# Attention of a four-layer hybrid model: GpSimd takes the low parts of half of each weight chunk and the zero blocks

## The chip, the cores and the metric

The kernel runs on one core of a Trainium2 chip. The metric is the device time of one execution in microseconds (us), as the median of several runs; lower is better.

The names used below: TensorE (PE in the profile) multiplies matrices, VectorE (DVE) and ScalarE (ACT) work element by element, GpSimd (POOL) can do so too, and SyncE (SP) issues the transfers from HBM. Each engine takes its instructions strictly in the order of its own queue, and waits at an instruction until the semaphores that it names have been reached.

## The reference

A model of four layers over 256 rows of 1024 columns: mixers of three kinds (retention, a gated linear recurrence, latent attention, retention again), each followed by a layer norm, and an MLP with squared ReLU, also followed by a layer norm. The change touches the third mixer alone, the latent attention:

```python
def mla_mixer(x, positions, w_in, q_norm_g, kv_norm_g, w_uq, w_ukv, w_o):
    c_q, c_kv, k_pe = jnp.split(x @ w_in, [384, 640], axis=-1)
    q = (rms_norm(c_q, q_norm_g) @ w_uq).reshape(B, S, 8, 192)
    q = jnp.concatenate([q[..., :128], rope(q[..., 128:], positions)], -1) * (192 ** -0.5)
    kv = (rms_norm(c_kv, kv_norm_g) @ w_ukv).reshape(B, S, 8, 256)
    k_nope, v = kv[..., :128], kv[..., 128:]
    k = jnp.concatenate([k_nope, broadcast(rope(k_pe, positions))], -1)
    ...                      # causal softmax(q k^T) v for each of 8 heads
    return o @ w_o
```

## The kernel before

**Numbers in two parts.** All arrays are 32-bit floats. For TensorE each operand x is split into a high part (a cast to the engine's own 32-bit format, `fp32r`) and a low part, x minus the high part. A product is then three products, added up in PSUM: high x high, high x low, low x high (`mm3`, L148 to L150). So each weight that comes from HBM costs a cast and a subtraction before it can be used. `split` (L141) does both: ScalarE casts (L142), VectorE subtracts (L143).

**Weight chunks.** `chunk` (L122) loads a piece of a weight array into one of three `raw` tiles (128 partitions x up to 2048 columns) by one transfer from SyncE's queue, and splits it into one of five `hl` tiles in two halves, first the first half of the columns, then the second. A `raw` tile can be loaded again only when both subtractions of the chunk that it held are done. In the attention a key/value chunk (`mla_ukv`, two of them) and an output chunk (`mla_o`, four) have 2048 columns, so halves of 1024; the chunk for the rotary part of the queries (`mla_uqr`, `wqr` in the code) and the two for the rest of the queries (`mla_uqn`, called uqn0 and uqn1 here) have 1536, so halves of 768. The chunks of the projection (`mla_in`, four) have 1408, halves of 704. `self.hold` orders a weight subtraction on VectorE behind an operation of the layer norm.

**The attention, `mla` (L686).** Rows come in two tiles t of 128. `down(t, i)` projects (tiles `low`) and normalises: ScalarE squares and sums (L719), VectorE scales the sum (`ve`, L165), GpSimd raises it to the power -1/2 (`rs`, L166, `rstd`), VectorE multiplies (`cn`, L721) and, for i = 0, adds the rotary terms of the keys (L726 to L730). `turn(t, i)` transposes `cn` on TensorE and splits it into `cT` (L744, L745). `values`, `keys` and `queries` make `vv`, `kn` and `qn` from `cT` and the chunks; `rope(t, w)` makes the rotary part of the queries (`qy`, then split as `qr`), and `turn_q` transposes it into `qpe`. `scores(h)` makes a head's scores `s` (L824) and its softmax (L826 to L830), `turn_p` transposes them into the tile `PT`, `attend` multiplies by the values (`oT`), and `out` multiplies by the output chunks into the accumulators `acc`. `PT` holds a block of zeros in each of its four parts (L704) for the half of the scores that the causal mask removes, and `kpe` two smaller ones (L706).

**What lies around it.** The end of the MLP before it (`close`) normalises both row tiles: the power for a row tile stands on GpSimd between the two steps L292 and L293 on VectorE. The transposes of row tile 1 (`flush`, L266) come between the projections of tile 0 and tile 1. GpSimd's only work in the whole kernel is the power of `rstd`, 36 times. The order on each engine is set by a scheduler that works on the code as it is written, so instructions of neighbouring steps are interleaved.

## Time and profile before

| | |
|---|---|
| median of 3 runs | 1321.05 us (1320.05 to 1322.92) |
| the profiled execution | 1322.59 us |
| its span, first to last instruction | 1320.8 us |
| mean granted TensorE clock | 0.997 of full speed |
| busy: TensorE, VectorE, ScalarE, GpSimd | 1303.6, 956.6, 658.9, 26.0 us |
| attention, about | 667 to 747 us of the span |

The profile shows one execution. Times inside it count from the span's start. A busy TensorE is not one at its peak, as products overlap and their ends are modelled; idle time in front of a product, with what released it, is what tells of lost time. In a row of the timeline, start and duration come first, in brackets behind it the idle time of the engine just before and what ended it; rows of the same kind are merged (x2, x3), with the time from the first start to the last end and the shape of the first of them.

### The profile page before, as it was taken

How to read it: one execution, taken by the hardware profiler on the slowest of the kernel's cores; microseconds unless marked ns; L12 is line 12 of the kernel's file. 1: busy time of each engine (PE TensorE's matmuls, PEld its weight loads, DVE VectorE, ACT ScalarE, POOL GpSimd, SP SyncE). 2: the span in 40 equal slices, each digit the busy share in tenths (PEclk: the TensorE clock that was granted, in tenths of full speed). 3: DMA queues.
4: the chain of work that ended last, by engine and by line, in shares of the span. 5: the costliest groups of instructions: out<-in, count | busy, mean ns of one | idle time of the engine just before them, and what ended most of it. 6: DMA issues, size and time to landing. Idle time of an engine off the chain costs nothing.

```text
span 1320.8 us, 17993 instructions
## 1 busy us (share of the span) xinstructions
PE 1303.6 (99%) x7130; PEld 1130.1 (86%) x7130; DVE 956.6 (72%) x1490; ACT 658.9 (50%) x1026; POOL 26.0 (2%) x40
## 2 busy tenths in 40 slices
PE   9999999999999999999999999999999999999997
PEld 6888888888889978888888888888898888888886
DVE  6976678766678988666589886666786657876664
ACT  5654445444438945444357554444444445454440
POOL 0000000000000000000010000000000000000000
PEclk9999999999999999999999999999999999999999
DMA  7745544655544366555435365555554544465540
GB/s 286 285 163 191 187 164 160 225 193 190 193 159 166 128 238 240 191 192 191 151 114 203 130 237 192 191 191 192 186 206 174 188 156 177 154 236 189 194 143 32
DMA packets 37281, 243.59 MB, mean 184 GB/s; under 512 B 4311, under 2 KB 4812, under 8 KB 10188
## 3 DMA queue, kind: packets, MB, share of 16 engines
q1 hardware_dynamic: 37196, 242.43, 51.8%
q8 instruction: 56, 0.92, 0.3%
q14 instruction: 29, 0.24, 0.1%
HBM read 241.36 MB, written 1.05 MB: 184 GB/s over the span
## 4 chain that ended last, share of the span: by engine, by line
PE 90%; DVE 5%; ACT 3%; issue 1%; DMA 0%; SPq 0%; POOL 0%; DVEq 0%; POOLq 0%; ACTq 0%
PE wk L960 14%; PE acc L148 12%; PE acc L150 12%; PE acc L149 12%; PE wk L148 10%; PE wk L150 10%; PE wk L149 10%; PE wk L962 8%; DVE hl L143 2%; PE wk L266 1%; ACT hl L142 1%; PE wk L428 1%; DMA raw<-ret_vg 0%; PE wk L984 0%; DVE Q L615 0%
## 5 line engine op out<-in xcount | busy, mean ns | idle before, releaser
L143 DVE TENSOR_TENSOR hl<-raw,hl 128x1024 fp32r<-128x1024 f32 (+3 forms) x448 | 526.3, 1196 | 176.8 <-ACT hl L142 173.8
L142 ACT CAST hl<-raw 128x1024 fp32r<-128x1024 f32 (+3 forms) x448 | 447.0, 1033 | 307.7 <-PE acc L150 174.1
L148 PE MATMUL acc<-hl,hT 128*128 128x512 f32 x512 | 200.5, 392 | 0.0
L149 PE MATMUL acc<-hl,hT 128*128 128x512 f32 x512 | 200.1, 391 | 0.0
L150 PE MATMUL acc<-hl,hT 128*128 128x512 f32 x512 | 199.2, 389 | 0.0
L960 PE MATMUL wk<-xT,hl 128*128 128x512 f32 x832 | 197.6, 390 | 0.0
L960 PEld LDWEIGHTS wk<-xT,hl 128*128 128x128 f32 x832 | 155.9, 188 | 32.3
L148 PE MATMUL wk<-hl,xT 128*128 128x512 f32 (+1 forms) x432 | 159.0, 368 | 0.3 <-ACT xT L142 0.3
L149 PE MATMUL wk<-hl,xT 128*128 128x512 f32 (+1 forms) x432 | 157.0, 364 | 0.2 <-DVE hl L143 0.2
L150 PE MATMUL wk<-hl,xT 128*128 128x512 f32 (+1 forms) x432 | 157.0, 364 | 0.0
L948 ACT COPY tb<-wk 128x256 f32<-128x256 f32 x104 | 38.8, 373 | 156.3 <-PE wk L962 156.3
L150 PEld LDWEIGHTS acc<-hl,hT 128*128 128x128 f32 x512 | 96.1, 188 | 20.3
L148 PEld LDWEIGHTS acc<-hl,hT 128*128 128x128 f32 x512 | 96.3, 188 | 18.5
L149 PEld LDWEIGHTS acc<-hl,hT 128*128 128x128 f32 x512 | 96.3, 188 | 17.9
L962 PEld LDWEIGHTS wk<-xT,hl 128*128 128x128 f32 x832 | 106.7, 191 | 4.1
L962 PE MATMUL wk<-xT,hl 128*128 128x256 f32 x832 | 107.9, 283 | 0.0
L949 DVE TENSOR_TENSOR s<-wk,tb 128x256 f32<-128x256 f32 x104 | 44.1, 424 | 80.5 <-ACT tb L948 76.8
L148 PEld LDWEIGHTS wk<-hl,xT 128*128 128x128 f32 x432 | 81.7, 189 | 14.8 <-ACT xT L142 2.6
L150 PEld LDWEIGHTS wk<-hl,xT 128*128 128x128 f32 x432 | 81.6, 189 | 14.0 <-DVE xT L143 1.6
L149 PEld LDWEIGHTS wk<-hl,xT 128*128 128x128 f32 x432 | 81.9, 190 | 12.8 <-DVE hl L143 1.1
L150 PE MATMUL wk<-xT,hl 128*128 128x256 f32 x288 | 81.6, 284 | 0.1
L148 PE MATMUL wk<-xT,hl 128*128 128x256 f32 x288 | 81.5, 283 | 0.0
(231 smaller groups left out, 1786.0 us busy)
## 6 DMA issues: line engine op xcount, KB each, us to landing
raw<-mlp SPq DMA_DIRECT2D x64, 1024.0 KB, 4.8
raw<-mlp_1b SPq DMA_DIRECT2D x56, 1024.0 KB, 4.8
raw<-ret_vg SPq DMA_DIRECT2D x30, 1024.0 KB, 4.8
raw<-ret_qk SPq DMA_DIRECT2D x16, 1024.0 KB
raw<-ret_o SPq DMA_DIRECT2D x16, 1024.0 KB, 5.0
raw<-lru_in SPq DMA_DIRECT2D x10, 1024.0 KB, 4.8
raw<-mlp_1a SPq DMA_DIRECT2D x8, 1024.0 KB
raw<-lru_o SPq DMA_DIRECT2D x5, 1024.0 KB, 4.7
```

The costliest lines, as they stand in the source:

```text
L142: self.nc.scalar.copy(out=hi, in_=x)
L143: return self.nc.vector.tensor_sub(out=lo, in0=x, in1=hi.bitcast(F32))
L148: mm(out, lhsT=st[0], rhs=mv[0], start=start, stop=False)
L149: mm(out, lhsT=st[0], rhs=mv[1], start=False, stop=False)
L150: mm(out, lhsT=st[1], rhs=mv[0], start=False, stop=stop)
L266: nc.tensor.transpose(ps[:, k * 128:k * 128 + 128], self.h[t][:, (j * 4 + k) * 128:(j * 4 + k + 1) * 128], self.idn)
L428: nc.tensor.transpose(tp[:, b * 128:b * 128 + 128], Y[h, t][:, b * 128:b * 128 + 128], self.idn)
L948: nc.scalar.copy(out=tb, in_=ps_lo)
L949: nc.vector.tensor_add(out=s, in0=ps_hi, in1=tb)
L960: mm(ps[b], lhsT=w[:, 0, k, f], rhs=xT[:, k], start=k == 0, stop=False)
L962: mm(ps[b][:, 256:], lhsT=w[:, 1, k, f], rhs=xT[:, k, 0], start=False, stop=k == 7)
```

## The change

`chunk` and `split` get an argument that puts the subtraction of a chunk's last half on GpSimd; the cast stays on ScalarE and the first half on VectorE. All nine chunks of the attention behind the projection use it: two key/value, three query and four output chunks. A subtraction on GpSimd isn't ordered behind the layer norm (`hold`). The six zero blocks are written by GpSimd too.

```diff
--- before.py
+++ after.py
@@ -119,7 +119,9 @@
         return [[self.acc.tile([128, 512], F32, name=f"acc{t}{n}", tag=f"acc{t}{n}") for n in range(2)]
                 for t in range(2)]
 
-    def chunk(self, src, k, n, pieces=2, loads=1, hold=True, mid=None):
+    def chunk(self, src, k, n, pieces=2, loads=1, hold=True, mid=None, pool=False):
+
+
 
         nc = self.nc
         raw = self.raw.tile([128, 2048], F32, name="raw", tag="raw")
@@ -133,14 +135,15 @@
                 mid()
         step = w // pieces
         for a in range(0, w, step):
-            lo = self.split(hl[:, 0, a:a + step], hl[:, 1, a:a + step], raw[:, a:a + step])
-            if hold and self.hold:
+            by = nc.gpsimd if pool and a + step == w else None
+            lo = self.split(hl[:, 0, a:a + step], hl[:, 1, a:a + step], raw[:, a:a + step], by)
+            if hold and self.hold and not by:
                 self.after(lo, self.hold)
         return hl[:, :, :w].rearrange("p s (k n) -> p s k n", n=n)
 
-    def split(self, hi, lo, x):
+    def split(self, hi, lo, x, by=None):
         self.nc.scalar.copy(out=hi, in_=x)
-        return self.nc.vector.tensor_sub(out=lo, in0=x, in1=hi.bitcast(F32))
+        return (by or self.nc.vector).tensor_sub(out=lo, in0=x, in1=hi.bitcast(F32))
 
     def mm3(self, out, st, mv, start, stop):
 
@@ -701,9 +704,9 @@
             vv = [p.tile([128, 2, MH * MV], F32R, name=f"vv{t}") for t in range(2)]
             for n in range(2):
                 for s in range(2):
-                    nc.vector.tensor_scalar_mul(out=PT[n][:, s, :128], in0=self.idn, scalar1=0.0)
+                    nc.gpsimd.tensor_scalar_mul(out=PT[n][:, s, :128], in0=self.idn, scalar1=0.0)
             for t in range(2):
-                nc.vector.tensor_scalar_mul(out=kpe[64:, 1, t * 128:t * 128 + 128], in0=self.idn[64:], scalar1=0.0)
+                nc.gpsimd.tensor_scalar_mul(out=kpe[64:, 1, t * 128:t * 128 + 128], in0=self.idn[64:], scalar1=0.0)
             CN, QN, R, P, OT = {}, {}, {}, {}, {}
 
             def down(t, i):
@@ -778,7 +781,7 @@
                 nc.scalar.copy(out=qpe[u][:, :, t * 128:t * 128 + 128], in_=ps.rearrange("p (h i) -> p h i", h=4))
 
             def kv_load(u):
-                return self.chunk(wkv[u], 2, 1024)
+                return self.chunk(wkv[u], 2, 1024, pool=True)
 
             def values(u, w, t):
                 c = slice(t * 128, t * 128 + 128)
@@ -852,7 +855,7 @@
                 self.proj(acc, t, terms, n == 0, n == MH // 2 - 1, ns)
 
             def out_load(n):
-                return self.chunk(wo[n], 2, 1024)
+                return self.chunk(wo[n], 2, 1024, pool=True)
 
             wi = [self.chunk(win[u], 2, 704, hold=False) for u in range(4)]
             tables()
@@ -867,14 +870,14 @@
             kn = self.xp.tile([128, 2, MH, 256], F32R, name="kn", tag="xT")
             turn(1, 0)
             values(0, w[0], 0)
-            wr = self.chunk(wqr, 3, 512)
+            wr = self.chunk(wqr, 3, 512, pool=True)
             rope(0, wr)
             w.append(kv_load(1))
             values(1, w[1], 0)
             turn(1, 1)
             acc = self.accs()
             rope(1, wr)
-            wq = [self.chunk(wqn[0], 3, 512)]
+            wq = [self.chunk(wqn[0], 3, 512, pool=True)]
             keys(0, w[0], 0)
             turn_q(0, 0)
             turn_q(0, 1)
@@ -889,7 +892,7 @@
             scores(1)
             queries(1, wq[0])
             keys(1, w[1], 0)
-            wq.append(self.chunk(wqn[1], 3, 512))
+            wq.append(self.chunk(wqn[1], 3, 512, pool=True))
             scores(2)
             turn_p(0)
             scores(3)
```

The order of the instructions on the engines follows. On GpSimd, at the place in the program where the attention begins and after it (`rs` are the powers, `PT` and `kpe` the zero blocks, `hl` the weight halves), before:

```order
L1049 MEMSET const-uint8-127 128x1
L1053 UNCONDITIONAL_BRANCH
L166 ISA
L166 TENSOR_TENSOR rs<-ve,mhalf 128x1 x36
L1053 UNCONDITIONAL_BRANCH
```

and now (the first 15 powers end with that of row tile 0 in the layer norm before the attention):

```order
L169 TENSOR_TENSOR rs<-ve,mhalf 128x1 x15
L707 TENSOR_SCALAR PT_5979<-idn 128x128 x2
L707 TENSOR_SCALAR PT_5980<-idn 128x128 x2
L709 TENSOR_SCALAR kpe<-idn 64x128 x2
L146 TENSOR_TENSOR hl<-raw,hl 128x1024
L169 TENSOR_TENSOR rs<-ve,mhalf 128x1 x4
L146 TENSOR_TENSOR hl<-raw,hl 128x768
L146 TENSOR_TENSOR hl<-raw,hl 128x1024
L169 TENSOR_TENSOR rs<-ve,mhalf 128x1
L146 TENSOR_TENSOR hl<-raw,hl 128x768 x2
L146 TENSOR_TENSOR hl<-raw,hl 128x1024 x4
L169 TENSOR_TENSOR rs<-ve,mhalf 128x1 x16
```

The zero blocks and the half of the first key/value chunk stand ahead of the power of row tile 1 in that layer norm and of three powers of the projections; the halves of `wqr` and of the second key/value chunk stand ahead of the last power of the projections, `down(1, 1)`.

On VectorE, from the `ve` of `down(1, 1)` to the split of the first rotary queries (`cn<-low_6180` is the normalised product of `down(1, 1)`, `vv` the values, `qy` and `qr` the rotary queries), before:

```order
L165 TENSOR_SCALAR ve<-ss 128x1
L745 SCALAR_TENSOR_TENSOR cT<-wk,cols,cT 128x128
L721 TENSOR_SCALAR cn<-low_6180,rs 128x384
L143 TENSOR_TENSOR vv_5986<-wk,vv_5986 128x512
L745 SCALAR_TENSOR_TENSOR cT<-wk,cols,cT 128x128
L143 TENSOR_TENSOR hl<-raw,hl 128x1024
L741 TENSOR_TENSOR kpe<-wk,kpe 64x128
L764 TENSOR_TENSOR qy<-wk,tab 128x512
L767 TENSOR_TENSOR qy<-wk,tab 128x8x32 x2
L143 TENSOR_TENSOR vv_5986<-wk,vv_5986 128x512
L768 TENSOR_TENSOR qy<-qy 128x512
L745 SCALAR_TENSOR_TENSOR cT<-wk,cols,cT 128x128
```

and now:

```order
L168 TENSOR_SCALAR ve<-ss 128x1
L748 SCALAR_TENSOR_TENSOR cT<-wk,cols,cT 128x128
L724 TENSOR_SCALAR cn<-low_6180,rs 128x384
L146 TENSOR_TENSOR hl<-raw,hl 128x768
L748 SCALAR_TENSOR_TENSOR cT<-wk,cols,cT 128x128
L146 TENSOR_TENSOR vv_5986<-wk,vv_5986 128x512
L744 TENSOR_TENSOR kpe<-wk,kpe 64x128
L767 TENSOR_TENSOR qy<-wk,tab 128x512
L770 TENSOR_TENSOR qy<-wk,tab 128x8x32 x2
L146 TENSOR_TENSOR hl<-raw,hl 128x768
L771 TENSOR_TENSOR qy<-qy 128x512
L146 TENSOR_TENSOR vv_5986<-wk,vv_5986 128x512
```

The key/value half is gone from between, the first halves of uqn0 and uqn1 stand ahead of `qy` and of its last step, and one `cT` has moved behind `qr`, which before was followed by it and a half.

On ScalarE, behind the squares of `down(1, 1)`, before:

```order
L142 CAST hl<-raw 128x768
L740 CAST kpe<-wk 128x128
L142 CAST hl<-raw 128x768
L142 CAST vv_5986<-wk 128x512
L744 ACTIVATE cT<-wk,cols 128x128
L142 CAST hl<-raw 128x768
L142 CAST qr<-qy 128x4x64 x2
```

and now:

```order
L145 CAST hl<-raw 128x768
L743 CAST kpe<-wk 128x128
L145 CAST hl<-raw 128x768 x2
L145 CAST vv_5986<-wk 128x512
L747 ACTIVATE cT<-wk,cols 128x128
L145 CAST qr<-qy 128x4x64 x2
```

Both casts of uqn1 (the `hl` behind `kpe`) now stand ahead of `vv` and of the first `cT` of `turn(1, 1)`; before, one stood behind them.

## Rows read from the trace of the kernel before

**Rows 1.** The page's first part: busy us (share of the span), instructions.

```profile
PE 1303.6 (99%) x7130; PEld 1130.1 (86%) x7130; DVE 956.6 (72%) x1490; ACT 658.9 (50%) x1026; POOL 26.0 (2%) x40
```

**Rows 2.** Windows: stretch, length, each engine's busy us (instructions), clock, DMA.

```profile
664.00:745.00 81.00, 77.23 (x508) 70.47 (x507) 72.83 (x162) 52.95 (x115) 3.12 (x5) 1.00 0.50 172
```

**Rows 3.** TensorE's waits, 640 to 780: us, times, longest.

```profile
PE wk L148 <- ACT cT L744: 0.9, 1, 0.9
PE wk L150 <- DVE qn L143: 0.8, 1, 0.8
PE wk L835 <- DVE s L830: 0.7, 1, 0.7
PE wk L736 <- DVE cn L721: 0.5, 1, 0.5
```

**Rows 4.** VectorE's groups by shape, 640 to 780: busy us, mean ns.

```profile
L143 DVE TENSOR_TENSOR hl<-raw,hl 128x1024 fp32r<-128x1024 f32 x28 | 33.5, 1216 | 2.8 <-ACT hl L142 2.8
...
L143 DVE TENSOR_TENSOR hl<-raw,hl 128x768 fp32r<-128x768 f32 x6 | 5.6, 948 | 0.0
...
L704 DVE TENSOR_SCALAR PT<-idn 128x128 fp32r<-128x128 f32 x4 | 0.8, 207 | 0.0
...
L706 DVE TENSOR_SCALAR kpe<-idn 64x128 fp32r<-64x128 f32 x2 | 0.4, 222 | 0.0
```

**Rows 5.** Timeline of GpSimd, 668 to 690: start, us.

```profile
669.67 0.92 POOL L166 TENSOR_TENSOR rs<-ve,mhalf 128x1 f32<-128x1 f32 x1 [8.44 <-DVE ve L165]
675.07 0.55 POOL L166 TENSOR_TENSOR rs<-ve,mhalf 128x1 f32<-128x1 f32 x1 [4.48 <-DVE ve L165]
...
688.25 0.55 POOL L166 TENSOR_TENSOR rs<-ve,mhalf 128x1 f32<-128x1 f32 x1 [4.45 <-DVE ve L165]
```

**Rows 6.** Timeline of VectorE, 666 to 690.

```profile
669.44 1.41 DVE L292 SCALAR_TENSOR_TENSOR h<-h,mv,lng 128x512 f32<-128x512 f32 x2
670.76 1.41 DVE L293 SCALAR_TENSOR_TENSOR h<-h,rs,lnb 128x512 f32<-128x512 f32 x2
...
684.82 0.35 DVE L730 TENSOR_TENSOR cn<-ky 128x64 f32<-128x64 f32 x2
...
687.96 0.14 DVE L165 TENSOR_SCALAR ve<-ss 128x1 f32<-128x1 f32 x1
...
688.83 0.62 DVE L721 TENSOR_SCALAR cn<-low,rs 128x384 f32<-128x384 f32 x1 [0.47 <-POOL rs L166]
```

**Rows 7.** GpSimd's groups in the whole span: busy us, mean ns, idle before.

```profile
L166 POOL TENSOR_TENSOR rs<-ve,mhalf 128x1 f32<-128x1 f32 x36 | 25.8, 716 | 1290.0 <-DVE ve L165 1290.0
```

**Rows 8.** Timeline of TensorE, 675 to 698.

```profile
675.80 1.03 PE L266 MATMUL wk<-idn,h 128*128 128x128 f32 x8
...
693.17 0.50 PE L148 MATMUL wk<-hl,cT 128*128 128x512 f32 x1 [0.95 <-ACT cT L744]
...
695.87 0.60 PE L777 MATMUL wk<-idn,qr 128*128 128x128 f32 x4
```

**Rows 9.** Timeline of ScalarE, 682 to 692.

```profile
683.15 3.47 ACT L142 CAST hl<-raw 128x768 fp32r<-128x768 f32 x4 [0.24 <-PE low L150]
...
691.15 0.83 ACT L142 CAST hl<-raw 128x768 fp32r<-128x768 f32 x1 [0.54 <-DMA raw<-mla_uqn]
```

**Rows 10.** Timeline of VectorE, 689 to 696.

```profile
689.37 0.68 DVE L143 TENSOR_TENSOR vv<-wk,vv 128x512 fp32r<-128x512 f32 x1
...
690.22 1.22 DVE L143 TENSOR_TENSOR hl<-raw,hl 128x1024 fp32r<-128x1024 f32 x1
...
695.21 0.75 DVE L143 TENSOR_TENSOR qr<-qy,qr 128x256 fp32r<-128x256 f32 x2
```

**Rows 11.** Timeline of SyncE's queue, 680 to 698: issues of transfers.

```profile
682.82 4.44 SPq L131 DMA_DIRECT2D raw<-mla_uqn  x2
```

**Rows 12.** Timeline of VectorE, 709 to 714.

```profile
709.67 2.35 DVE L143 TENSOR_TENSOR hl<-raw,hl 128x1024 fp32r<-128x1024 f32 x2
...
713.25 0.69 DVE L143 TENSOR_TENSOR qn<-wk,qn 128x512 fp32r<-128x512 f32 x1
```

## The prediction

> **What bounds the kernel now.** The page comes first: TensorE is busy 99% of the span [rows 1]. So time can only come out of the places where TensorE waits, and the change can only reach those of the attention. In the window that holds it, 664 to 745 us, TensorE is busy 77.23 of 81 us, VectorE 72.83 and GpSimd 3.12, at a granted clock of 1.00 throughout [rows 2]: TensorE idles 3.8 us there, and that is the most the change can win (0.29% of the span). The view of who waited for whom names four waits of half a microsecond or more: 0.9 us for ScalarE's cT, and 0.8, 0.7 and 0.5 us for VectorE's qn, s and cn [rows 3]. VectorE releases these last three, 2.0 us, so it is the engine to relieve; but each of them is a place in an order, not a share of its load.
>
> **What leaves VectorE.** Nine second halves: six of 1024 columns at 1.216 us and three of 768 at 0.948, 10.1 us; and six zero blocks, 4 x 0.207 + 2 x 0.222 = 1.3 us [rows 4]. Together 11.4 us of its 72.8.
>
> **What GpSimd gets.** The trace holds no wide operation of GpSimd. Its only one, the power of one column in rstd, takes 0.55 us while VectorE stands idle for it [rows 5], where VectorE's one-column ve takes 0.14 [rows 6]. Bounds for a 1024-column half: no faster than VectorE's own 1.21 us, and no worse than that times 0.55/0.14, about 4.7 us. I take 2.3 us, near their geometric middle, and by the same factor 1.8 us for 768 columns (bounds 0.95 and 3.7): 19 us of work for an engine that idles 78. A zero block lies between VectorE's 0.2 us and the power's 0.55; I take 0.3. The Trainium skill (GPSIMD Engine Reference, Performance versus the Vector engine) calls GpSimd the wrong engine for elementwise work and gives 4.497 us for a two-input add of 2048 columns against VectorE's 2.293; scaled to 1024 columns that is an estimate of 2.25 us, and by it the sum below stays as it is. No row here shows it.
>
> **Do the two engines block each other?** GpSimd's 36 powers [rows 7] fall in two kinds: 16 take 0.92 us, all in layer norm while VectorE runs L292 on two SBUF inputs (h and the gain), and 20 take 0.55, while VectorE waits for their result [rows 5]. The one at 669.67 began 0.23 us after a pair of L292 did, each of which takes 0.7 us, and ended at 670.59, half a microsecond after the first of the pair [rows 6]. That is what a held port looks like. A half on GpSimd reads two SBUF tiles, as do the first halves left on VectorE, the second step of qy, the splits of qr and the sums into cn; operations on PSUM operands would not clash. I take sharing as the likelier case. The Trainium skill (SBUF — State Buffer, Who interferes with whom) says that a VectorE instruction with two SBUF inputs and a GpSimd one that reads SBUF exclude each other for the whole instruction. By that rule the time is the +1.7 us below, without it rival A's -1.8; the 0.92 against 0.55 agrees with it, but shows only GpSimd as the one that waits.
>
> **Place one, the start (667 to 679).** GpSimd's queue now holds the zero blocks and the half of the first key/value chunk ahead of the power for row tile 1 of the layer norm, which began at 669.67 [rows 5]. From about 667.5, when the MLP's last product ends: six zeros 1.8, half 2.3, power 0.9, so it ends near 672.5 instead of 670.59, and the two L293 behind it near 674.0 instead of 672.17 [rows 6]. Next late would be the power of the first projection at 675.07 [rows 5] and TensorE's transposes of that tile at 675.80 [rows 8]: the cover left is 0.8 us, and a half of over 3.1 us uses it up. On the other side, the last projection half no longer stands behind the layer norm on VectorE, and cn can come up to 0.5 us sooner [rows 3]. I take 0, with -0.7 and +1.0 as ends.
>
> **Place two, the queries (684 to 700).** ScalarE's four casts begin at 683.15 [rows 9]; the second of wqr ends near 684.8, the second of the other key/value chunk at 686.6. GpSimd makes these two halves before the power that began at 688.25 [rows 5]. With nothing shared: 684.8 + 1.8 + 2.3 + 0.55 = 689.45 for its end, 0.65 late. With sharing, VectorE's first halves and sums into cn, 0.95 + 1.21 + 0.35 [rows 4, 6], lie end to end with GpSimd's 4.1: 684.8 + 6.6 + 0.55, about 692.0, and cn behind it is done at 692.6 instead of 689.45 [rows 6]. VectorE stands still for it in either case, and all that leads to the turned qr is queued behind it. Before, that took 6.6 us, from vv at 689.37 to the end of qr at 695.96 [rows 10]; less the key/value half (1.22) and plus the first half of uqn1 that now stands there (0.95), it is 6.3 us. Nothing shared: 690.1 + 6.3 = 696.4, 0.4 late. Shared: 692.6 + 6.3 = 698.9, plus between 0 and 3.0 us (VectorE's two-input part of it) for GpSimd's two uqn halves; I take 0.3, near the low end since VectorE's PSUM operations fit beside GpSimd's halves, and get 699.2: **+3.2**, for TensorE, which turned qr at 695.87 [rows 8], waits there. TensorE's wait for cT moves too, inside these 3.2: the transfer of uqn1 needs wqr's raw buffer, which GpSimd frees near 686.6 to 687.6 (it was issued at 682.82 + 4.44 - 0.33 = 686.93 [rows 11], and ScalarE waited for it until 691.15 [rows 9]), and both uqn1 casts now stand ahead of vv and cT on ScalarE, so TensorE goes on at 693.4 to 694.4 instead of 693.17 [rows 8]. SP's later transfers and ScalarE's casts that wait for GpSimd to give up a buffer are those of the output chunks; the scores cover them.
>
> **Place three, the scores (711 to 714).** VectorE ran two weight halves of an output chunk at 709.67, and qn came only at 713.25 [rows 12]; TensorE stood 0.7 and 0.8 us for s and qn [rows 3]. One of the two halves goes, like all second halves before it, and TensorE itself comes 3.2 us later. Both waits go: **-1.5**. What is late next is TensorE, since none of the four waits lies behind this place.
>
> **Sum:** 0 + 3.2 - 1.5 = +1.7 us. The profiled run took 1322.59 us for a span of 1320.8; the median of the three is 1321.05, 1.54 less. I put the difference on the median: **1322.7 us**.
>
> **Rivals.** *A, nothing is shared.* Place one gives -0.7, place two +0.4, place three -1.5: -1.8, 1319.25 us. For it: the trace shows only GpSimd waiting, and half of VectorE's operations there read PSUM. Against: the 0.92 us. At the ceiling of 3.8 us it would be 1317.25. *B, GpSimd's queue becomes the bound.* If a 1024 half takes 4.7 and a 768 half 3.7 us and a zero 0.55, the first power ends near 676.4 and the chain of rstd and cn moves by 3 us; at place two 684.8 + 3 + 3.7 + 4.7 + 0.55 = 696.75, cn 697.4, qr 703.7, so +7.7 - 1.5 = +6.2, 1327.25 us. It decides from about 3.1 us for a 1024 half, where the cover of place one ends. For it: 0.55 us for one column; against: much of that must be fixed cost. *C, it does nothing.* The halves all come in time, but TensorE's next limit at each place is ScalarE's cT or a transfer, so that what is won at one is stood out at the next: 1321.05 us.
>
> **How the numbers follow.** About 0.2% (2.6 us) is what a measurement of this kernel can tell from no change. Forecast (shared, +1.7): 0.48, of which 0.35 within that bound, 0.12 slower and 0.01 faster. A: 0.32, of which 0.17 faster and 0.15 within, since its centre is close to the bound and its ceiling beyond it. B: 0.15, of which 0.14 slower. C: 0.05, within. Sums: faster 0.18, same 0.56, slower 0.26. The range, 1318.0 to 1325.6, goes from 1.2 us under A's centre to the forecast with all 3.0 us of sharing at place two, and leaves out most of B and the best end of A.
>
> **What would show it.** In the changed profile: GpSimd's 1024 halves near 2.3 us (over 3.1: B); VectorE's two-input operations stretched, or never beside a half of GpSimd (neither: A); the last power of the attention beginning near 691.5 (689: A); TensorE waiting over a microsecond before the first turn of qr; and no wait for s and qn around 711 to 717. The forecast is wrong if VectorE does not stretch, if qr comes in time, or if place three keeps its waits.

## The result, and the profile after

| | before | after |
|---|---|---|
| median | 1321.30 us (5 runs, 1320.05 to 1322.92) | 1327.97 us (5 runs, 1327.44 to 1329.58) |
| ratio | | 1.0052, interval 1.0040 to 1.0063 |
| profiled execution, its span | 1322.59, 1320.8 us | 1327.52, 1325.7 us |

The change makes the kernel 6.7 us slower. The forecast was 1322.7 us with a range of 1318.0 to 1325.6 and chances of 0.18 for faster, 0.56 for the same and 0.26 for slower: the time lies outside the range, on the side that had 0.26.

In the two profiled executions all of the difference lies in the attention. A good ruler there is GpSimd's own work: from the start of the power of row tile 0 in the layer norm ahead of it to the start of the first power behind it. In this document that is called the stretch. It leaves out what runs before and behind. GpSimd's timeline (start, us, engine, line, operation; idle time before it in brackets), before:

```profile
660.30 0.92 POOL L166 TENSOR_TENSOR rs<-ve,mhalf 128x1 f32<-128x1 f32 x1 [168.38 <-DVE ve L165]
...
750.98 0.92 POOL L166 TENSOR_TENSOR rs<-ve,mhalf 128x1 f32<-128x1 f32 x1 [62.19 <-DVE ve L165]
```

and after, which answers to [rows 5]:

```profile
659.79 0.92 POOL L169 TENSOR_TENSOR rs<-ve,mhalf 128x1 f32<-128x1 f32 x1 [168.37 <-DVE ve L168]
666.99 2.54 POOL L707 TENSOR_SCALAR PT<-idn 128x128 fp32r<-128x128 f32 x4 [6.27 <-PE acc L153]
...
671.00 2.47 POOL L146 TENSOR_TENSOR hl<-raw,hl 128x1024 fp32r<-128x1024 f32 x1
673.44 0.57 POOL L169 TENSOR_TENSOR rs<-ve,mhalf 128x1 f32<-128x1 f32 x1
...
685.27 4.62 POOL L146 TENSOR_TENSOR hl<-raw,hl 128x768 fp32r<-128x768 f32 x2 [1.07 <-ACT hl L145]
691.32 0.55 POOL L169 TENSOR_TENSOR rs<-ve,mhalf 128x1 f32<-128x1 f32 x1 [1.42 <-DVE ve L168]
...
705.25 2.69 POOL L146 TENSOR_TENSOR hl<-raw,hl 128x1024 fp32r<-128x1024 f32 x1 [6.39 <-ACT hl L145]
708.68 2.39 POOL L146 TENSOR_TENSOR hl<-raw,hl 128x1024 fp32r<-128x1024 f32 x1 [0.75 <-ACT hl L145]
...
755.84 0.99 POOL L169 TENSOR_TENSOR rs<-ve,mhalf 128x1 f32<-128x1 f32 x1 [25.82 <-DVE ve L168]
```

The stretch was 750.98 - 660.30 = 90.68 us and is 755.84 - 659.79 = 96.05: 5.4 us longer (everything before it runs 0.5 us earlier in this execution, so the spans differ by 4.9). TensorE is busy 86.91 us of it before and 87.36 after, so what grew is its idle time, from 3.8 to 8.7 us. Line numbers after are three higher than before.

What TensorE stood for, 640 to 780 us, in the view of who waited for whom (us, times, longest), answers to [rows 3]:

```profile
PE wk L739 <- DVE cn L733: 3.1, 1, 3.1
PE wk L153 <- DVE qn L146: 1.7, 1, 1.7
PE wk L780 <- DVE qr L146: 1.5, 2, 0.8
PE wk L739 <- DVE cn L724: 1.4, 2, 0.9
PE wk L151 <- ACT cT L747: 0.7, 1, 0.7
...
```

With a wait of 0.2 us for qpe that is 8.6 us, where it was 3.7. The longest wait is new: for L733, the sums of the rotary terms into `cn`, which before lasted 0.35 us [rows 6] and held up nobody. The wait for qn is the old one at place three, twice as long; the one for s is gone.

VectorE lost 11.4 us of work, yet its busy time in the attention hardly fell: 72.41 us in a window of 88 us, where it was 72.83 in one of 81 [rows 2], and over the whole stretch 79.77 us, where it was 80.62. In the windows view (stretch, length, each engine's busy us and instructions, clock, DMA):

```profile
664.00:752.00 88.00, 79.31 (x516) 71.42 (x514) 72.41 (x148) 54.20 (x117) 28.76 (x20) 1.00 0.47 161
```

The timeline of VectorE says where the relief went. Five of its rows, all of operations on two SBUF inputs:

```profile
674.04 1.41 DVE L296 SCALAR_TENSOR_TENSOR h<-h,rs,lnb 128x512 f32<-128x512 f32 x2 [2.81 <-POOL rs L169]
...
685.83 4.15 DVE L733 TENSOR_TENSOR cn<-ky 128x64 f32<-128x64 f32 x2
...
697.69 1.79 DVE L146 TENSOR_TENSOR qr<-qy,qr 128x256 fp32r<-128x256 f32 x2
...
706.44 2.11 DVE L146 TENSOR_TENSOR qr<-qy,qr 128x256 fp32r<-128x256 f32 x2
...
709.08 3.08 DVE L146 TENSOR_TENSOR hl<-raw,hl 128x1024 fp32r<-128x1024 f32 x1
```

The first waits for GpSimd's queue: its own length is that of before, but VectorE stood 2.81 us for the power that the zero blocks and a half put off to 673.44. The other four are stretched: the sums from 0.35 to 4.15 us, qr from 0.75 [rows 10] to 1.79 and 2.11, a weight half from 1.21 to 3.08. Each lies beside a half of GpSimd. What TensorE then stands for, in its own timeline, is the end of the stretched ones (of the last of them by way of the qn that is queued behind it):

```profile
690.03 0.33 PE L739 MATMUL wk<-idn,cn 128*128 128x128 f32 x1 [3.10 <-DVE cn L733]
...
699.20 0.66 PE L780 MATMUL wk<-idn,qr 128*128 128x128 f32 x4 [0.83 <-DVE qr L146]
...
708.27 1.09 PE L780 MATMUL wk<-idn,qr 128*128 128x128 f32 x8 [0.65 <-DVE qr L146]
712.81 0.39 PE L153 MATMUL wk<-kn,qn 128*128 128x256 f32 x1 [1.71 <-DVE qn L146]
```

### The profile page after: what moved, and what is told of

It is laid out like the page before. It is cut to its first block, busy times and chain, and to the rows that moved or that the text cites. A ratio compares the mean times of both kernels' runs of the same rounds, so it can differ in the third digit from the quotient of the medians.

```text
span 1325.7 us, 18007 instructions
## 1 busy us (share of the span) xinstructions
PE 1303.9 (98%) x7130; PEld 1129.8 (85%) x7130; DVE 956.1 (72%) x1475; ACT 659.9 (50%) x1026; POOL 51.8 (4%) x55
## 4 chain that ended last, share of the span: by engine, by line
PE 91%; DVE 4%; ACT 3%; issue 1%; POOL 1%; DMA 0%; SPq 0%; DVEq 0%; POOLq 0%; ACTq 0%
PE wk L963 14%; PE acc L151 12%; PE acc L153 12%; PE acc L152 12%; PE wk L151 10%; PE wk L153 10%; PE wk L152 10%; PE wk L965 8%; DVE hl L146 1%; PE wk L269 1%; ACT hl L145 1%; PE wk L431 1%; DMA raw<-ret_vg 0%; PE wk L987 0%; DVE Q L618 0%
## 5 line engine op out<-in xcount | busy, mean ns | idle before, releaser
L146 DVE TENSOR_TENSOR hl<-raw,hl 128x1024 fp32r<-128x1024 f32 (+3 forms) x439 | 518.4, 1202 | 177.0 <-ACT hl L145 173.8
```

The lines of the kernel that those rows point to most:

```text
L146: return (by or self.nc.vector).tensor_sub(out=lo, in0=x, in1=hi.bitcast(F32))
```

## The experiments

Two theories. **S**, sharing: a GpSimd half and a VectorE operation on two SBUF inputs exclude each other, so VectorE stands while GpSimd works. **Q**, the queue: nothing is shared, but GpSimd's long operations stand ahead of its powers, for which VectorE waits.

**The operations by themselves.** The stages of this kernel are fenced off from each other; in each, GpSimd and VectorE run a row of operations on tiles in SBUF (or one in PSUM) that don't depend on each other.

```diff
+ psub(3); psub(2, 768); psub(2, 256)       # GpSimd subtracts, alone
+ vsub(3); vps(3); vsc(3); vrd(3)           # VectorE alone: two SBUF inputs, PSUM + SBUF, one input, reduce
...
+ psub(4); vsub(8)                          # side by side
+ psub(4); vps(16)
+ psub(4); vsc(24)
+ psub(4); vrd(16)
+ [memset x 8 on GpSimd]; vsub(8)
+ [product with a constant x 4 on GpSimd]; vsub(8)
```

> The whole model is left out: the kernel loads x, times operations on it in stages that are fenced off from each other, and writes x out. Theory S (a GpSimd half and a VectorE operation on two SBUF inputs exclude each other): a GpSimd subtraction of 1024 columns alone takes 2.0 to 2.6 us, of 768 columns 1.5 to 1.9; a VectorE one 1.2 us alone. Side by side, four GpSimd subtractions (9 us) and eight of VectorE (9.6 us) take together 18 to 20 us, the sum of both, while beside VectorE operations that read PSUM neither side is stretched by more than 10%. Theory Q (nothing is shared, only GpSimd's queue is long): every pair of stages takes as long as its longer side, about 10 us, and each operation lasts what it lasts alone. Zero blocks by a product on GpSimd: 0.6 us for 128 columns by both; a memset is the open point: S would leave VectorE's two-input subtractions unstretched beside it if reading is what clashes.

In the one run of it, GpSimd alone took, by shape, 2338 ns for a subtraction of 1024 columns, 1799 for 768, 951 for a memset of 1024, 530 for a zero block of 128 columns and 2767 for the same product of 1024. VectorE's 8 subtractions would take 9.3 us alone, the spacing being 1.16. Side by side, GpSimd's timeline:

```profile
34.92 13.22 POOL L101 TENSOR_TENSOR g<-h,h 128x1024 fp32r<-128x1024 f32 x4 [0.19 <-SPq L113]
52.80 9.27 POOL L101 TENSOR_TENSOR g<-h,h 128x1024 fp32r<-128x1024 f32 x4 [4.66 <-SPq L115]
62.58 10.02 POOL L101 TENSOR_TENSOR g<-h,h 128x1024 fp32r<-128x1024 f32 x4 [0.52 <-SPq L117]
...
88.99 7.20 POOL L122 MEMSET m<- 128x1024 f32 x8 [0.30 <-SPq L121]
98.25 12.10 POOL L124 TENSOR_SCALAR g<-h 128x1024 fp32r<-128x1024 f32 x4 [2.06 <-SPq L123]
```

and VectorE's of the same stages:

```profile
34.88 17.75 DVE L102 TENSOR_TENSOR o<-h,h 128x1024 fp32r<-128x1024 f32 x8 [9.45 <-SPq L113]
52.76 9.66 DVE L103 TENSOR_TENSOR o<-q,h 128x512 fp32r<-128x512 f32 x16
62.54 16.72 DVE L104 TENSOR_SCALAR o<-h 128x512 fp32r<-128x512 f32 x24
...
88.96 9.17 DVE L102 TENSOR_TENSOR o<-h,h 128x1024 fp32r<-128x1024 f32 x8
```

The first pair takes 17.8 us where the two rows alone take 9.3 + 9.3: S, if a little under its 18 to 20. While GpSimd worked, VectorE finished four of its subtractions, at a mean of 3357 ns, which is about one of each in turn: each waits for nearly the whole of the other's instruction. Beside operations that read PSUM (the second stage) nothing is stretched, nor in the fourth, not among the rows, beside VectorE's reductions (680 ns each, 674 alone). The third stage was a surprise: a product with a constant, one SBUF input, went from 416 to 771 ns at the mean, 16.7 us for 24. And in the fifth GpSimd's writes, 7.20 us of them, cost VectorE's subtractions nothing: 9.17 us. The Trainium skill (SBUF — State Buffer, SBUF: two separate sides) calls the pair of ports that the two engines share an exclusive lock for the whole instruction, and says that a VectorE operation with two SBUF inputs takes it only against a GpSimd operation that reads SBUF. The first, second and fifth stage agree. In the sixth (the last row of GpSimd), it reads one input, and the two rows of 11.1 and 9.3 us (4 x 2767 ns, 8 x 1.16) were both done after 12.6 us (VectorE's mean 1637 ns, GpSimd's 3046): here most of the work overlapped, less than the whole instruction was excluded, and the measurement decides.

**All runs of the model** stand in one table. The ratio, with its 95% interval, is to the kernel before, run beside them on the same chip, and is not the quotient of the two medians; the stretch is the ruler from above, of one profiled execution (two of the changed kernel agree within 0.04 us); "clock" is what the stretch lost to a granted clock below 1 (the sum of 1 - clock over windows of 1 us); "waits" are TensorE's, 640 to 790 us.

| run | median us | ratio, interval | stretch | clock | waits |
|---|---|---|---|---|---|
| before | 1321.2 to 1322.0 | 1 | 90.68 | 0 | 3.7 |
| changed | 1327.97 | 1.0052, 1.0040 to 1.0063 | 96.05 | 0 | 8.6 |
| zeros alone | 1320.86 | 0.9992, 0.9984 to 1.0001 | 89.86 | 0 | 3.2 |
| halves alone | 1330.58 | 1.0069, 1.0057 to 1.0082 | 100.43 | 3.4 | 10.5 |
| without the pair wqr, key/value | 1324.66 | 1.0029, 1.0020 to 1.0038 | 92.99 | 0 | 6.2 |
| idle reads | 1335.20 | 1.0104, 1.0090 to 1.0118 | 104.53 | 6.8 | 10.9 |
| idle writes | 1322.03 | 1.0002, 0.9993 to 1.0011 | 90.55 | 0 | 3.4 |
| changed, no output halves | 1326.09 | 1.0034, 1.0021 to 1.0046 | 94.56 | 0 | 6.2 |
| zeros and output halves | 1319.37 | 0.9988, 0.9979 to 0.9997 | 88.98 | 0 | 2.1 |
| changed, sums first | 1328.92 | 1.0057, 1.0044 to 1.0070 | 98.29 | 3.4 | 8.2 |
| zeros, output and first key/value half | 1324.56 | 1.0025, 1.0017 to 1.0034 | 92.17 | 0 | 5.0 |
| zeros, output halves, a cast put back | 1323.16 | 1.0013, 1.0005 to 1.0022 | 91.33 | 0 | 4.0 |
| changed, again | 1327.55 | 1.0048, 1.0034 to 1.0062 | 96.09 | 0 | 8.5 |

**The same reads and the same queue, one without the other.** In both of these VectorE does all its work as before. GpSimd does work that nobody uses: in one it reads, in the other it only writes. The writes keep it busy for 21.4 us, the reads for 28.5; alone the reads would take about 22 us, an estimate from the 722 and 1799 ns that 256 and 768 columns took in the probe.

```diff
+ lo = self.split(hl[:, 0, a:a + step], hl[:, 1, a:a + step], raw[:, a:a + step])    # VectorE, both halves
+ # idle reads, behind the second half's cast, for each piece b:e of 384 columns (the loop is left out):
+ nc.gpsimd.tensor_sub(out=self.scr[:, :e - b], in0=raw[:, b:e], in1=hl[:, 0, b:e].bitcast(F32))
+ # idle writes, behind the same cast, 6 or 5 times (the loop is left out):
+ nc.gpsimd.memset(self.scr, 0.0)
```

> All nine halves and the zero blocks are made by VectorE as in the kernel before. Beside them, at the nine places of the change, GpSimd makes the same second half once more into a scratch tile that nobody reads (in pieces of 384 columns): it reads what the change lets it read, and takes as long, but no work leaves VectorE. S (two-input operations of the two engines exclude each other): VectorE's sums into cn last about 4 us, TensorE waits some 3 us for them, and the time is that of the run with the halves alone or worse, +8 to +12 us against the kernel before. Q (only GpSimd's queue ahead of its power counts): no operation of VectorE is longer than before, and the powers come up to 4 us late: +1 to +4 us.

> As the run with idle reads, but GpSimd writes zeros into the scratch tile in their place, each time once the cast of that second half is done, in as many pieces as make up about the same time (6 x 0.36 us for 1024 columns, 5 x 0.36 for 768, from 0.951 us for 1024 columns in the probe, where writes left VectorE's subtractions at 1.218 us). GpSimd's queue is as long as with the reads. S: no operation of VectorE is stretched, and the powers come at most 2 us late: 0 to +3 us against the kernel before. Q: as the idle reads, within 1 us. If reads and writes cost the same, GpSimd's queue is the cause and the shared port is not.

The reads cost 13.3 us, the writes 0.1 us. So what costs the time is that GpSimd reads, not that it is busy: S, not Q. There is one more difference between the two, that reads hold a chunk's `raw` and `hl` tiles longer; but between 660 and 765 us the view of the waits names no engine that waits for a transfer, in either run. At the same point of the program, GpSimd and VectorE with the idle reads:

```profile
688.02 7.26 POOL L142 TENSOR_TENSOR scr<-raw,hl 128x384 f32<-128x384 f32 x5 [1.13 <-issue]
```

```profile
688.18 5.43 DVE L149 TENSOR_TENSOR hl<-raw,hl 128x768 fp32r<-128x768 f32 x3
```

and with the idle writes:

```profile
684.63 4.24 POOL L141 MEMSET scr<- 128x384 f32 x9 [1.12 <-ACT hl L148]
```

```profile
684.80 2.96 DVE L149 TENSOR_TENSOR hl<-raw,hl 128x768 fp32r<-128x768 f32 x3
```

The same three halves take VectorE 5.43 us beside reads and 2.96 beside writes. (The shape in a merged row is that of its first.) The reads that VectorE holds up also make GpSimd's queue longer: VectorE then stands 1.89 us for the power behind them, 0.44 with the writes. The expectation missed two things. The sums into cn were not among the stretched here (0.35 us): in this order they stand ahead of GpSimd's first read. And the loss was above the 8 to 12 us given, since 6.8 us of it came from the clock, of which more below.

**One part alone.** First the zeros, then the halves.

```diff
- pool=True                               # zeros alone: no chunk hands a half to GpSimd
- nc.gpsimd.tensor_scalar_mul(out=PT...   # halves alone: the zero blocks on VectorE again
+ nc.vector.tensor_scalar_mul(out=PT...
```

> Only the six zero blocks go to GpSimd; all nine halves stay on VectorE. Both theories: the zeros take 2.54 + 1.31 = 3.85 us on GpSimd from about 667 us, so the power of the layer norm's second row tile starts near 670.9 to 671.5 instead of 669.67, which fits into the 0.8 us of cover at TensorE's transposes or passes it a little. S and Q both: 0 to +0.8 us against the kernel before, 1321.1 to 1322.1. If it costs 2 us or more, the zero blocks are a main term of the loss and the halves less of it.

> The nine halves on GpSimd, the six zero blocks on VectorE as in the kernel before. Both theories: the start gives back about 1 us of the loss, the queries keep theirs: +5.0 to +6.0 us against the kernel before, about 1326.5 to 1327. In the trace the sums into cn (two SBUF inputs) still last about 4 us beside two halves of GpSimd, and TensorE still waits about 3 us for them. If it comes out within 1 us of the kernel before, the zeros are the cause.

The zeros alone cost nothing; the stretch is 0.8 us shorter, since VectorE, without them, has the last projection half and cn ready sooner (TensorE's wait for cn goes from 0.5 to 0.2 us). The halves alone cost 9.2 us, not 5 to 6: more than with the zeros. The zeros had kept GpSimd busy until 671 and so held its first half back, past VectorE's work for the layer norm and the last projection half. Without them, the half starts while VectorE is at L295:

```profile
667.58 3.56 DVE L295 SCALAR_TENSOR_TENSOR h<-h,mv,lng 128x512 f32<-128x512 f32 x2
```

L295 takes 3.56 us instead of 1.41 [rows 6], the last projection half, which now stands behind it and the rest of the layer norm, ends at 674.4, and TensorE stands for it. In its timeline:

```profile
671.23 0.34 PE L152 MATMUL low<-hl,xT 128*128 128x384 f32 x1
674.48 0.64 PE L152 MATMUL low<-hl,xT 128*128 128x320 f32 x1 [2.91 <-DVE hl L146]
...
675.50 0.52 PE L151 MATMUL low<-hl,xT 128*128 128x384 f32 x1
```

The product of 384 columns takes 0.52 us behind the wait and 0.34 ahead of it. The windows view shows the granted clock at half (1.2 of 2.4 GHz) for most of these 4 us (0.57 at the mean); it fell again, to 0.66 at the mean from 690 to 695 us, around the second long wait, of 3.18 us:

```profile
674.00:678.00 4.00, 3.52 (x12) 3.50 (x13) 2.07 (x9) 0.47 (x2) 0.55 (x1) 0.57 0.63 217
```

**Without the pair.**

```diff
- return self.chunk(wkv[u], 2, 1024, pool=True)
+ return self.chunk(wkv[u], 2, 1024, pool=u == 0)
- wr = self.chunk(wqr, 3, 512, pool=True)
+ wr = self.chunk(wqr, 3, 512)
```

> As the changed kernel, but the second halves of wqr and of the second key/value chunk, the two that GpSimd makes back to back while VectorE adds into cn, are on VectorE again. S: the sums into cn last 0.35 us again, TensorE's wait of 3.1 us for them goes, the power of the second down projection comes near 688.7 and the turned qr near 696.5; left are about 1 us at the start and what the uqn and output halves cost: +2 to +3.5 us against the kernel before, 1323.3 to 1324.8. Q: the same halves leave GpSimd's queue ahead of the power, so Q expects a gain too, but only of the 3.1 us that qr is later (the power 691.3 instead of 688.3), and no change in how long VectorE's sums last. Where the 3.1 us wait in front of TensorE's third transpose stays, neither is right.

3.2 us slower than before by the median, within what S gave, and the sums last 0.35 us again. But part of this agreement is luck. The profiled execution, the fastest of the 11 (1322.37 us; the slowest took 1328.16, at a mean clock of 0.994), has a stretch only 2.3 us longer than before; the rest of the median goes with the clock, which S did not count. Nor did the saving come through the turned qr alone: GpSimd's second uqn half stretches the first qr to 1.81 us, an output half stretches the second step of qy to 2.89 us, and TensorE stands 2.3 us for qr and 2.1 us behind the transposes of turn(1,1).

**The pair held back.** Every engine's order is that of the changed kernel; only GpSimd waits for the sums before its two halves.

```diff
+ self.tc.add_manual_dep(lo.ins, self.sums.ins.name, ...)    # wqr's and the second key/value chunk's half on GpSimd
```

> As the changed kernel, in the same order on every engine, but GpSimd's two halves (wqr and the second key/value chunk) wait for VectorE's two sums into cn, so that these last 0.35 us again. Theory S with the forecast's chain: the wait of 3.1 us at TensorE's transposes of turn(1,0) goes, but the halves now end near 686.2 + 4.6 = 690.8, VectorE's key/value half still lies end to end with them, and the power of the second projection still comes near 691.5, so TensorE waits the same 3 us later, ahead of the turned qr: 1327 to 1328.5, the changed kernel within 1 us. Rival, the sums are themselves the loss: then about 3 us come back, 1324 to 1325.

The sums last 0.35 us and the wait of 3.1 us in front of turn(1,0) is gone, yet nothing comes back: 1328.92 us, a little above the 1327 to 1328.5 that was expected and 1.4 above the changed kernel on the same chip. Of its stretch 3.4 us stand as lost clock. GpSimd, then VectorE, then TensorE:

```profile
685.54 5.07 POOL L148 TENSOR_TENSOR hl<-raw,hl 128x768 fp32r<-128x768 f32 x2 [2.21 <-DVE cn L735]
690.56 0.55 POOL L171 TENSOR_TENSOR rs<-ve,mhalf 128x1 f32<-128x1 f32 x1
```

```profile
691.14 0.62 DVE L726 TENSOR_SCALAR cn<-low,rs 128x384 f32<-128x384 f32 x1 [3.81 <-POOL rs L171]
691.68 2.02 DVE L148 TENSOR_TENSOR hl<-raw,hl 128x768 fp32r<-128x768 f32 x1
...
693.88 0.67 DVE L148 TENSOR_TENSOR vv<-wk,vv 128x512 fp32r<-128x512 f32 x1
```

```profile
694.61 0.90 PE L741 MATMUL wk<-idn,cn 128*128 128x128 f32 x3 [3.23 <-DVE vv L148]
```

VectorE now stands 3.81 us for the power behind the two halves instead: that is Q. But TensorE's new wait of 3.23 us ends with vv, not with cn, and in between a first half of a uqn chunk lies beside GpSimd's next half and takes 2.02 us instead of 0.95. So about 1.1 us of that wait is sharing again. At place two the loss has two forms. Either VectorE's operations lie between the halves, or the power lies behind them; taking one away brought out the other, because the same 4 to 5 us of GpSimd stand on the way to cn(1,1). That the queue alone would cost as much is not shown.

**The output halves.** Taken out of the changed kernel, and put alone (with the zeros) on the kernel before.

```diff
- return self.chunk(wo[n], 2, 1024, pool=True)    # changed, no output halves
+ return self.chunk(wo[n], 2, 1024)
- pool=True                                       # zeros and output halves: on all but wo
```

> As the changed kernel, but the four halves of the output chunks are on VectorE again. If place three was lost to these halves (qr 2.11 us instead of 0.75 and hl 3.08 instead of 1.21 beside them), TensorE's waits of 0.65 us for qr and 1.71 for qn there give way to the 1.5 us that it stood in the kernel before: 0.5 to 1.5 us less than the changed kernel, 1326.5 to 1327.5. Rival: place three is lost because the queries come late from place two, and then it is the same time as the changed kernel, 1328 +-0.5, with VectorE's two halves of 1.2 us in the way of qn as before.

> Only the zero blocks and the four halves of the output chunks go to GpSimd. The forecast's step for place three, taken alone, says that the waits for s and qn (0.7 and 0.8 us) go: 1.5 us less than the run with the zeros alone, about 1319.4. Sharing says that the halves stretch VectorE's qr, s or hl there, and TensorE waits as long or longer than in the kernel before: 1320.9 to 1322.5. Places one and two are those of the run with the zeros alone by both.

Alone they win: 1319.37 us against 1320.86 for the zeros alone. What was expected by sharing, 1320.9 to 1322.5, was wrong here. The difference of the medians is the 1.5 us that the forecast gave these halves, but its size is not sure: the two ran on different chips, their ratios are 0.9988 and 0.9992 with intervals that overlap, and the stretch is only 0.9 us shorter. In that run's waits nothing is left for s or qn:

```profile
PE wk L151 <- ACT cT L747: 0.9, 1, 0.9
PE wk L780 <- DVE qr L146: 0.4, 1, 0.4
PE wk L780 <- ACT qpe L781: 0.4, 1, 0.4
...
```

Sharing shows there too, but it costs little. VectorE's qr lies beside a half and takes 1.46 us instead of 0.75, for which TensorE stands 0.4 us; the next half takes GpSimd itself 3.50 us instead of 2.4, and TensorE waits for none of that:

```profile
699.52 1.46 DVE L146 TENSOR_TENSOR qr<-qy,qr 128x256 fp32r<-128x256 f32 x2
```

```profile
703.50 3.50 POOL L146 TENSOR_TENSOR hl<-raw,hl 128x1024 fp32r<-128x1024 f32 x1 [3.13 <-ACT hl L145]
```

In the changed kernel they lose: without them the stretch is 1.5 us shorter and the median 1.5 to 1.9 us lower than the changed kernel's two, a little more than the 0.5 to 1.5 expected. There TensorE comes late to the scores, so the waits of before are gone at place three without any help, and only the stretched qr, hl and qn remain. The run with zeros and output halves is the fastest of all, 0.9988 of the time before (interval 0.9979 to 0.9997).

**Two attempts that failed.** Putting the first key/value half back on GpSimd, on top of the fastest run; and, in another, holding a uqn cast on ScalarE behind a `cT`.

```diff
- return self.chunk(wkv[u], 2, 1024)
+ return self.chunk(wkv[u], 2, 1024, pool=u == 0)                     # first key/value half
- wq = [self.chunk(wqn[0], 3, 512)]
+ wq = [self.chunk(wqn[0], 3, 512, behind=TC[1, 0])]                  # a cast put back
```

> The zero blocks, the four output halves and the half of the first key/value chunk on GpSimd; wqr, the second key/value chunk and both uqn chunks on VectorE. Forecast's step for place one: the half costs nothing there, -0.7 to +1.0. The trace of the changed kernel says that the power behind it comes 2.5 us later and TensorE stands 0.5 us longer for cn than in the kernel before, and 1.2 us longer than with the zeros alone: about +1 us against the run with zeros and output halves, 1320.4. If it is as fast as that run, place one costs nothing.

> As the run with the zero blocks and the output halves on GpSimd, which is the fastest so far, but on ScalarE the first cast of the first uqn chunk, which waits for its transfer, may not run before the first scaled copy of turn(1,1). If TensorE's wait of 0.9 us for cT there is the price of that cast's place in the queue, it goes: 1318.5. If cT is late for another reason, nothing: 1319.4, or up to 1 us slower, since the chunk's casts then fall beside those of qr and qpe.

Both expectations were missed, 1324.56 us instead of 1320.4 and 1323.16 instead of 1318.5 to 1320.4, since both edits moved the order of other instructions. With the key/value half, cn comes 1.2 us later in all (its waits 1.4 instead of 0.2), as expected; but ScalarE then runs the second cast of a uqn chunk (690.81) and one of vv (691.55) ahead of the `cT` that the product behind the transposes of turn(1,1) needs, where in the fastest run that cast came behind it, and TensorE stands 2.08 us there:

```profile
692.02 0.38 ACT L747 ACTIVATE cT<-wk,cols 128x128 fp32r<-128x128 f32 x1
```

```profile
692.46 0.50 PE L151 MATMUL wk<-hl,cT 128*128 128x512 f32 x1 [2.08 <-DVE hl L146]
```

The row names VectorE's hl, which ended last (at 692.43), but the cT ended at 692.40, three hundredths earlier: which of the two it was can't be told from the row. That the median is 3.4 us above before, with a stretch only 1.5 us longer, goes with the clock: its profiled execution is the fastest of its runs (1321.76 us at a mean clock of 0.999), and most others ran at 0.995 to 0.997. The held cast brought a new wait of 2.2 us for qn and left 1.3 us for cT, in two waits.

**The changed kernel again.**

> The changed kernel itself, beside the others on this chip: 1328 +-1 by every theory. Open is where the other 1.3 us of the difference between the medians (6.7) are, of which the two profiled runs show 5.4 in the attention: if TensorE's long waits make the clock fall there in other runs of it, a second profile may show a stretch at 0.5 of the granted clock between 690 and 715 us, which the first did not have; if not, it lies in which runs lose 1.7 us to the clock at 470 us, outside the attention.

Its second profile is the first one once more, stretch 96.09 us, no fall of the clock in the attention. The medians differ by more than the stretch, 6.3 to 6.7 against 5.4 us. At a mean granted clock of 0.999 this kernel took 1325.97 and 1326.45 us (2 runs), the kernel before 1320.20 to 1321.88 (9 runs, median 1320.59): 5.6 us, the stretch's difference. The changed kernel's two slowest runs here, 1329 us, had a clock of 0.995 and 0.996, and none of the 21 runs of before was below 0.997. So the last microsecond goes with a clock that falls more often. That it falls behind TensorE's new waits, in runs that were not profiled, is likely from the runs with halves alone, idle reads and the pair held back, but not shown for the changed kernel itself.

## Why the prediction was wrong, point by point

**What bounds the kernel, and that VectorE's relief is worth little by itself:** right. VectorE lost 11.4 us of work and its busy time over the stretch fell by 0.9.

**Prices.** A 1024 half was put at 2.3 us and took 2.34 alone and 2.45 in the kernel; a 768 half at 1.8, and took 1.80 alone, 2.53 in the kernel with its waits. The zero blocks were put at 0.3 us and took 0.65 (2.54 us for the four of PT), twice as much: the upper bound of 0.55, taken from an operation on one column, was no upper bound.

**Sharing:** right, and the reads-and-writes pair shows it as cause. The 0.92 against 0.55 us of the powers [rows 5, 7] fits it: in the changed kernel the power at 673.44, for which VectorE stands idle, takes 0.57 us where it took 0.92 beside L292. The forecast saw it only for two SBUF inputs; the one-input product from SBUF is stretched too.

**Place one,** forecast 0 (-0.7 to +1.0): TensorE's waits there went from 0.7 to 1.4 us, +0.7. The power ended at 674.01, not 672.5, because of the zeros' price. Inside the bounds.

**Place two,** forecast +3.2: TensorE's waits between 684 and 704 went from 1.5 to 4.8 us, +3.3. The power ended at 691.87 (forecast 692.0), cn at 692.5 (692.6), and TensorE turned qr at 699.20 (699.2). But most of the wait stood somewhere else than the forecast had it: 3.1 us in front of turn(1,0), because the sums into cn, 0.35 us long, each waited for a half of GpSimd. The two one by one, of which the first ends with GpSimd's half of wqr (685.27 + 2.32 us) and the second with that of the key/value chunk (687.56 + 2.33):

```profile
685.83 1.85 DVE L733 TENSOR_TENSOR cn<-ky 128x64 f32<-128x64 f32 x1
```

```profile
687.60 2.37 DVE L733 TENSOR_TENSOR cn<-ky 128x64 f32<-128x64 f32 x1
```

The forecast had these sums in its chain only for what is queued behind them and not for who reads them. It cost nothing in the sum, since TensorE, once late, met the late qr with 0.83 us of wait, not the over 1 us that the forecast named as its sign; the run with the pair held back shows the exchange. That qr is hit to the tenth is partly luck: beside the uqn halves it lasted 1.0 us longer than before, where 0.3 was taken for them. And the forecast let TensorE go on behind cT at 693.4 to 694.4, where it went on at 696.22, 3.7 us behind cn as before.

**Place three,** forecast -1.5: this step failed. TensorE's waits there went from 1.5 to 2.4 us, +0.9, so the term is wrong by 2.4 us, the largest error of the sum. The mechanism that it names is right: with the queries in time, the output halves on GpSimd take both waits away (0.9 us less of the stretch, 1.5 by the medians), and with the queries late the waits for s and qn go by themselves (6.2 us of waits without the output halves, none of them there). What the step left out is that the output halves take the port too. It had counted sharing at place two and none at place three, where qr (2.11 us), hl (3.08) and behind them qn lay beside GpSimd's halves from 705.25 to 711.07.

**The sum, and the step to the median.** The terms give +1.7, the waits +4.9 (0.7 + 3.3 + 0.9), the stretch +5.4, of which 0.45 is TensorE's busy time; the medians differ by 6.7. The forecast put its sum on the median of before, and so took it that both kernels lose the same to the clock. The two profiled executions do: each lost about 1.7 us to a clock of half near 470 us, ahead of the attention. But that of before lay 1.3 us above the median of its five runs, and that of after 0.45 us below. So a further 1.3 us of the miss, the 6.7 less the 5.4, goes with a clock that falls more often in the changed kernel, which the forecast had put at nothing.

**Rivals.** A (nothing shared) is refuted by the reads and by the probe. B (GpSimd's queue) gave 1327.25 us, nearly the time, but for another reason: it needed halves of over 3.1 us, and they took 2.45. Its mechanism does appear, in the kernel where the pair is held back. C (no change) fell: the time moved by 6.7 us. A time that agrees with a rival does not confirm it.

## What to carry to other kernels

Work that is moved from VectorE to GpSimd did not relieve VectorE here where VectorE meanwhile read two inputs from SBUF (or, as the product in the probe, one). Two sums of 0.35 us together, for which somebody waited, became 4 us long between two halves, so look at each short operation beside the moved one and ask who reads it. What could be moved here was work at a point where TensorE's next operands do not hang on VectorE's two-input operations or on GpSimd's own chain (the output halves with the zero blocks, 0.9988 of the time); work that only writes cost 0.1 us. Where a mechanism is assumed, apply it at every place of the sum, not only at the one where it came to mind.

## What the runs showed of the hardware that was not expected

- GpSimd's writes left VectorE's two-input subtractions alone: eight memsets of 0.95 us beside eight subtractions left these at 1218 ns, and 21.4 us of them in the attention cost 0.1 us, where the reads cost 13.3. A zero block, one input from SBUF to SBUF, did take VectorE 0.38 us beside them instead of 0.22 (idle writes, at 671.68).
- A VectorE product with a constant, SBUF to SBUF, went from 416 to 771 ns beside GpSimd's subtractions.
- On GpSimd a product with a constant, one input of 1024 columns, took 2767 ns, more than the two-input subtraction's 2338. The Trainium skill (GPSIMD Engine Reference, Engine selection) calls one-input operations there roughly line-rate; this one was not.
- The granted clock fell to half for 3.4 us and more around or behind waits of TensorE of 2.9 and 3.2 us (halves alone) and 3.2 us (pair held back), not behind the 3.1 us in both profiles of the changed kernel. With the idle reads it also fell behind three waits of 0.7 to 0.8 us within 3 us. Of the 13.9 us by which the idle reads made the stretch longer, 6.8 us stand as lost clock.
